# The S5 parameters of a hybrid encoder layer: scratch memory of their own, and a place at the head of the program

## The chip, the cores and the metric

The kernel runs on one core of a Trainium2 chip. The time is that of one execution on the device, in microseconds (us). The engines are TensorE (PE, with its weight loads PEld), VectorE (DVE), ScalarE (ACT), GpSimd (POOL) and SyncE (SP), which issues most transfers. Before the change the median of 3 runs is 1712.62 us (1712.08 to 1717.11).

## What is computed

One layer of a hybrid trunk, for 1024 tokens of a prompt and 32 of a decoded sample, with a width of 1024, all in float32:

```python
h = rmsnorm(x, prm['ln_mix_g'])
z = h @ prm['w_in'] + prm['b_in']                  # mLSTM q k v o i f | attention q k v | S5 u
y_a = head_rmsnorm(jax.nn.sigmoid(o_a) * mlstm(q_a, k_a, v_a, i_a, f_a, c0, n0, m0), prm['gn_a_g'], 4)
y_b = head_rmsnorm(stick_breaking(q_b, k_b, v_b), prm['gn_b_g'], 6)
y_s, s_re, s_im = s5(u_c, prm, s0_re, s0_im)
g = jax.nn.gelu(y_s)
y_c = rmsnorm(g * jax.nn.sigmoid(g @ prm['w_glu'] + prm['b_glu']), prm['gn_c_g'])
x = x + concat(y_a, y_b, y_c) @ prm['w_out']
x = x + cross_attn(rmsnorm(x, prm['ln_x_g']), mem_k, mem_v, prm['w_xq'], prm['w_xo'])
x = x + conv_ffn(rmsnorm(x, prm['ln_ffn_g']), prm, conv_prev)
```

S5 is a diagonal state space model of 16 groups with 64 complex states each and 16 channels. Before it can run, its parameters have to be prepared: from `ssm_a_re`, `ssm_a_im` and `ssm_log_dt` come the step, the magnitude, the sine and cosine of each state's rotation, the first 8 powers of the transition and the rotation squared ten times over; `ssm_b` is scaled with these and `ssm_c` is transposed.

## The kernel before, in words

**Stages.** The nine x tiles (eight of 128 tokens, one of 32) are normed, transposed by PE and split into a high and a low part; each dense product is three matmuls with the halves of both operands. The input projection runs over blocks of 128 output columns and three chunks of tokens. Its first three blocks (u, u, and the gates) run chunk by chunk, so that PE can begin on chunk 0 with three x tiles; the others run block by block, in the order attention 0 and 1, mLSTM 0 and 1, attention 2, mLSTM 2. Then come the keys and values of the memory, `w_out`, the cross attention and the FFN (from about 960 us on).

**The order of the work.** The main stream is those dense products. Beside it run side streams, written as generators: the norms of the x tiles, the parameter columns (`vec_late`, line 638), S5 with its GLU (`s5`, line 1331, `glu`, line 1619), the norm of the memory (`lend`, line 1687), the attention (`stick`) and the mLSTM (`mlstm`, line 1099). A planner (lines 62 to 259) keeps a clock for each engine and a cost for each instruction; after each step of the main stream, `advance` asks every side stream in turn, and one whose inputs are ready by the planner's clock emits its next step. A transfer costs 0.5 us of one shared issue resource and 0.65 us and its bytes at 360 GB/s. All instructions go through one helper, so the profile gives nearly all of them line 173. Behind the planner a scheduler of the compiler places instructions once more, by a simulation of its own: one that was written later but has its operands can go ahead.

**Gates.** S5's groups need u in DRAM; the mLSTM preface needs the gates and `s5_done` (line 1100), its chunks need all twelve mLSTM blocks (line 1202); `w_out` needs attention, S5 and the first mLSTM chunks (line 2065).

**Memory.** `m_s5` (line 533) is a stretch of 8896 columns. x tiles 4 to 8 lie in it from column 3000 on (line 582). `s5` waits until all nine x tiles are normed (line 1332), frees the stretch and takes it again: 2560 columns for the small parameters (`sc`), the rest for the large tiles (`sw`). The raw parameters `pr` and `h0` and the scratch `tq`, `tq2`, `tb` lie in the tile `ot`, and the raw `ssm_c` in `W1`; those are columns in which x tiles lay. `s5`, `vec_late` and the others are added after the eighth step of the first dense blocks (line 1710). `vec_late` loads 11 rows of gains, biases and convolution weights, yields once, and transposes them to the columns `vecC` and `vecB`.

**In the trace**, S5's tiles, x tiles 4 to 8 and the mLSTM's are all `zy`, x tiles 0 to 3 and the attention's `zf`, the split tokens `zb` (high) and `za` (low), and the PSUM tiles `mm`, `tp` and `gp`.

Of the kernel before, what the change touches and what calls it, by code (L numbers as in the profile page):

```python
# [7 lines left out]
F32 = mybir.dt.float32  # L8
# [7 lines left out]
P = 128  # L16
D = 1024
# [10 lines left out]
SG, SC, SP_ = 16, 16, 64  # L28
# [5 lines left out]
NB = TA // 8  # L34
NP_ = T // 8
S5_W = 8896
OUT_AT = [0, 416, 800, TA]
SAMPLE_AT = 2
DEPTH = 4
# [7 lines left out]
SLACK = [-0.25, 1, -0.5]  # L47
# [6 lines left out]
def tile_fn(tc, *args):  # L54
# [7 lines left out]
    clk = {"pe": 0.0, "act": 0.0, "dve": 0.0, "pool": 0.0, "sp": 0.0}  # L62
# [25 lines left out]
    def width(x):  # L88
        n = 1
        for d in x.shape[1:]:  # L90
            n *= d
        return n
# [39 lines left out]
    class Timed:  # L132
        def __init__(self, eng, key):
            self.eng, self.key = eng, key
# [43 lines left out]
    g = Timed(nc.gpsimd, "pool")  # L178
    pe = Timed(nc.tensor, "pe")
# [49 lines left out]
    def add(x, at=None, slack=0.0):  # L229
        sd = x if isinstance(x, Window) else Side(x, chain[0], slack)  # L230
        sides.insert(len(sides) if at is None else at, sd)
        return sd

    def advance():
        for sd in list(sides):
            sd.run()
            if sd.done:
                sides.remove(sd)
# [7 lines left out]
    def until(cond):  # L246
        while not cond():
            t = clk["pe"]
            advance()
            if clk["pe"] == t and not cond():  # L250
                clk["pe"] += 0.25
                assert clk["pe"] < 1e4, "nothing moves"
# [8 lines left out]
    with ExitStack() as top:  # L261
# [34 lines left out]
        class Mem:  # L296
# [39 lines left out]
            def tile(self, shape, dt=F32):  # L336
                x = self.view(shape, dt, self.at)
                self.at += (width(x) + 7) // 8 * 8
                return x
# [26 lines left out]
        def const(shape, dt=F32, name="c"):  # L366
            return cpool.tile(shape, dt, name=name)
# [155 lines left out]
        for gi, grp in enumerate(GROUPS):  # L523
            for n in DOWN if gi == 0 else range(KD):
# [7 lines left out]
        sp = Bag({"ss": (4, 8), "stg": (3, IN_W), "sthl": (2, 2 * IN_W, "R"), "nat": (1, 9 * P)})  # L532
        m_s5 = Mem(S5_W)
        xb = Bag({"g": (1, D), "xt": (4, D), "ur": (2, 8 * NB), "vr": (2, P), "graw": (1, KD * 64),
                  "ghl": (1, KD * P, "R"), "mhl": (2, KD * P, "R")})


        ident = const([P, P], name="ident")
# [40 lines left out]

        xn = [0]  # L580
        gmix = xb.tile([P, D], "g")
        xts = [xb.tile([P, D], "xt") if i < 4 else m_s5.view([P, D], F32, 3000 + (i - 4) * D) for i in range(9)]

        def x_load(i, eng):
            n = P if i < 8 else TS
# [2 lines left out]
        def x_tile(i):  # L588
            yield from norm_T(None, P if i < 8 else TS, gmix, h_hi, h_lo, i * P, xts[i])
            xn[0] = i + 1  # L590
# [14 lines left out]
        ra, rb = xb.tile([P, P], "vr"), xb.tile([88, P], "vr")  # L605
# [32 lines left out]
        def vec_late():  # L638
            at = 0
            for key, ap in (("b_glu", a["b_glu"][0]), ("gn_a", a["gn_a_g"][0]), ("gn_b", a["gn_b_g"][0]),  # L640
                            ("gn_c", a["gn_c_g"][0]), ("ln_x", a["ln_x_g"][0]), ("ln_ffn", a["ln_ffn_g"][0]),
                            ("ln_f", a["ln_f_g"])):
                VA[key] = at
                at = rows(ra, at, ap)
            at = 0
            for j in range(3):
                at = rows(rb, at, a["ffn_conv_w"][0, j])
            rows(rb, at, a["ffn_conv_b"][0])
            yield
            pa, pb = gp(), gp()  # L650
            pe.transpose(pa[:, :34], ra[:34], ident[:34, :34])
            pe.transpose(pb[:, :88], rb, ident[:88, :88])
            v.tensor_copy(vecC, pa[:, :34])
            v.tensor_copy(vecB, pb[:, :88])
            late.append(1)
            yield
# [664 lines left out]
        def cmul(o_r, o_i, ar, ai, br, bi, t0, t1, g_=None):  # L1321
# [6 lines left out]
            v.tensor_tensor(out=o_r, in0=o_r, in1=t0, op=ALU.subtract)  # L1328
            g_.tensor_tensor(out=o_i, in0=o_i, in1=t1, op=ALU.add)

        def s5():
            while xn[0] < 9:
                yield
            G = 4
            tt, ts2 = v.tensor_tensor, v.tensor_scalar
            m_s5.free()
            m_sc, m_sw = Mem(2560), Mem(S5_W - 2560)
            sc, sw = m_sc.tile, m_sw.tile
            tc_, tsn = sw([P, G, NB]), sw([P, G, NB])
            uK, xp, GC, GS = (sw([P, G, NB]) for _ in range(4))  # L1340
            VT, ot, VTt, VJt, W1, TT = (sw([P, G, P]) for _ in range(6))
            Ks = sw([P, G, SC])
            otv = ot.rearrange("p g n -> p (g n)")

            pr = otv[:48, 0:2 * SP_].rearrange("r (j p) -> r j p", j=2)
            for i, nm in enumerate(("ssm_a_re", "ssm_a_im", "ssm_log_dt")):
                for j in range(2):
                    s.dma_start(pr[16 * i:16 * i + 16, j, :], a[nm][0])
            h0 = otv[:32, 2 * SP_:4 * SP_].rearrange("r (j p) -> r j p", j=2)
            s.dma_start(h0[0:16, 0], a["state_ssm_re"][0, 0])  # L1350
            s.dma_start(h0[0:16, 1], a["state_ssm_im"][0, 0])
            s.dma_start(h0[16:32, 0], a["state_ssm_im"][0, 0])
# [3 lines left out]
            sy.dma_start(nA[64:P], a["ssm_b_im"][0].rearrange("g p c -> p g c"))  # L1356
            sy.dma_start(nB[0:64], a["ssm_b_im"][0].rearrange("g p c -> p g c"))
            sy.dma_start(nB[64:P], a["ssm_b_re"][0].rearrange("g p c -> p g c"))
            cn = W1.rearrange("p g n -> p (g n)").rearrange("p (h j i q) -> p h j i q", h=2, j=2, i=2)
            for hf in range(2):  # L1360
                rr = slice(8 * hf, 8 * hf + 8)
                for j, (x, y_) in enumerate((("ssm_c_re", "ssm_c_im"), ("ssm_c_im", "ssm_c_re"))):
# [58 lines left out]
            yield  # L1421

            Lr, Li = sc([P, 16, 9]), sc([P, 16, 9])
            tq = otv[:, 256:320].rearrange("p (g m) -> p g m", g=16)
            tq2 = otv[:, 320:384].rearrange("p (g m) -> p g m", g=16)
            g.memset(Lr[:, :, 0:1], 1.0)
            g.memset(Li[:, :, 0:1], 0.0)
            v.tensor_copy(Lr[:, :, 1], lr)
# [26 lines left out]

            ts2(nB[0:64], nB[0:64], -1.0, None, op0=ALU.mult)
            bA, bB = sc([P, 16, SC]), sc([P, 16, SC])
            tb = otv[:, 0:256].rearrange("p (g c) -> p g c", c=SC)
            bc = [P, 16, SC]
            zrb, zib = zr.unsqueeze(2).to_broadcast(bc), zi.unsqueeze(2).to_broadcast(bc)  # L1460
            tt(out=bA, in0=nA, in1=zrb, op=ALU.mult)
# [26 lines left out]
            fin = sc([P, 2, 2, 16])  # L1488
            X0, X0J = sc([P, 16]), sc([P, 16])
            yield  # L1490
            tE = [otv[:, 256 * i:256 * i + 256].rearrange("p (g n) -> p g n", g=G) for i in range(2)]
            for hf in range(4):
                gs = slice(G * hf, G * hf + G)
# [8 lines left out]
                for i in range(8):  # L1502
                    m = 1 << i
# [75 lines left out]
                for dst, tab in ((GC, tc_), (GS, tsn)):  # L1579
                    v.tensor_tensor(out=dst[:, :, 1:NB], in0=xp[:, :, 0:NB - 1], in1=tab[:, :, 0:NB - 1], op=ALU.mult)  # L1580
                    i = 0 if dst is GC else 1
# [28 lines left out]
            sy.dma_start(p_ssm_im[0, 0], fo[0:16, 64:P])  # L1610
            sy.dma_start(s_ssm_re[0, 0], fo[16:32, 0:64])
            sy.dma_start(s_ssm_im[0, 0], fo[16:32, 64:P])
            m_sc.free()
            m_sw.free()
            yield
            yield from glu()
            s5_done.append(1)
# [1 line left out]
        def glu():  # L1619
            mg = Mem(S5_W)  # L1620
            sg_ = mg.tile
# [56 lines left out]
        chunks = list(range(NCH))  # L1678
        h_free = []
        xw_ = add(Window((x_tile(i) for i in range(9)), 4))  # L1680
        until(lambda: xn[0] >= 1)
        W.prime(1)

# [11 lines left out]

        def later_sides():
            add(vec_late())
            add(s5(), slack=SLACK[0])
            add(lend())
            add(stick())  # L1700
            add(mlstm(), slack=SLACK[1])
# [671 lines left out]

        out_n = [OUT_AT[c + 1] - OUT_AT[c] for c in range(NCH)]
        early, stat_done, out_done = {}, [], []

        def os_(c):
            return slice(OUT_AT[c], OUT_AT[c + 1])

        def out_tiles(c):  # L2380
            end = min(OUT_AT[c + 1], T)
            t = [(t0, min(P, end - t0)) for t0 in range(OUT_AT[c], end, P)]
            return t + [(T, TS)] if c == NCH - 1 else t
# [137 lines left out]
```

## Time and profile before

| | |
|---|---|
| median of 3 runs | 1712.62 us |
| the profiled execution, its own time | 1716.38 us |
| its span in the trace | 1714.6 us |
| PE, PEld busy | 96%, 93% of the span |
| DVE, ACT, POOL busy | 66%, 44%, 27% |
| mean granted clock of PE | 0.987 |
| moved by the DMA engines | 229.91 MB, mean 134 GB/s |

The profile is that of one execution; its rows give the start of an instruction from the span's start, its time, engine, operation, tiles and shapes, and in brackets how long the engine had been idle before it and what ended that. The granted clock is the share of TensorE's full clock that the throttle let through.

### The profile page before, as it was taken

To read this page: it belongs to the slowest core of one execution; us is meant where nothing else is said; L and a number is where in the kernel's file an instruction comes from. 1 tells how busy PE (TensorE), PEld (TensorE's weight loads), DVE (VectorE), ACT (ScalarE), POOL (GpSimd) and SP (SyncE) were. 2 spreads that over 40 slices of the span, in tenths; PEclk is the share of its full clock that TensorE was granted. 3 is DMA by queue.
4 is the path that set the end of the run, shared out by engine and by line. 5 is a ranking of instruction groups with operands and counts; after the bars stand their busy time and mean duration, and the time that the engine had idled before them with its cause. 6 is when DMAs were issued, how large, how long until landed. Compare 5 with 4: busy or idle time off the path is not lost.

```text
span 1714.6 us, 30434 instructions
## 1 busy us (share of the span) xinstructions
PE 1642.7 (96%) x11616; PEld 1598.1 (93%) x11616; DVE 1137.3 (66%) x2209; ACT 753.6 (44%) x1480; POOL 463.2 (27%) x624
## 2 busy tenths in 40 slices
PE   5999999999999799999999989999999999999997
PEld 5989989999888799999999889999999999999997
DVE  6778878845796667766656698777777777333232
ACT  5434434534664555544444454444444445111143
POOL 4234335011214233200102546533333330000022
PEclk9999999999899999999999999999999999999999
DMA  7564544254479965455554555222222217332121
GB/s 216 146 161 115 138 109 105 78 158 133 124 232 257 253 200 162 125 170 178 171 167 124 159 158 169 94 76 89 86 75 75 76 63 240 127 100 75 43 69 65
DMA packets 328392, 229.91 MB, mean 134 GB/s; under 512 B 43564, under 2 KB 309707, under 8 KB 327991
## 3 DMA queue, kind: packets, MB, share of 16 engines
q1 hardware_dynamic: 309991, 214.57, 42.5%
q10 hardware_dynamic: 18256, 13.40, 2.6%
q8 instruction: 92, 1.51, 0.4%
q14 instruction: 53, 0.43, 0.1%
HBM read 170.95 MB, written 56.38 MB: 133 GB/s over the span
## 4 chain that ended last, share of the span: by engine, by line
PE 76%; DMA 9%; DVE 8%; issue 2%; ACT 2%; POOL 1%; SPq 1%; ACTq 0%; DVEq 0%; POOLq 0%
PE mm L173 47%; PE gp L173 19%; PE tp L173 10%; DVE zy L173 3%; DVE zf L173 2%; DVE zr L173 1%; DVE zx L173 1%; DMA d_mv<-zr 1%; DMA zf<-d_act 1%; SPq L173 1%; DVE w_lo L173 1%; DMA w_raw<-in_w_in_dram 1%; ACT zy L173 1%; DMA zy<-d_uu 1%; ACT zf L173 0%
## 5 line engine op out<-in xcount | busy, mean ns | idle before, releaser
L173 PE MATMUL mm<-zb,w_hi 128*128 128x352 f32 (+4 forms) x1234 | 366.5, 330 | 2.5 <-DVE zb L173 1.3
L173 PE MATMUL mm<-zr,w_hi 128*128 128x352 f32 (+2 forms) x1358 | 289.2, 312 | 8.4 <-ACT zf L173 4.1
L173 ACT ACTIVATE w_hi<-w_raw 128x1024 fp32r<-128x1024 f32 (+1 forms) x150 | 149.6, 997 | 284.5 <-PE mm L173 207.2
L173 PE MATMUL mm<-zb,w_lo 128*128 128x384 f32 (+2 forms) x826 | 273.6, 331 | 0.0
L173 POOL TENSOR_TENSOR zf<-zf 128x352 f32<-128x352 f32 (+5 forms) x98 | 118.5, 1210 | 566.5 <-ACT zf L173 484.8
L173 PE MATMUL mm<-zr,w_lo 128*128 128x264 f32 (+2 forms) x1058 | 235.9, 304 | 0.7 <-ACT zf L173 0.7
L173 PEld LDWEIGHTS mm<-zb,w_hi 128*128 128x128 f32 x1234 | 227.6, 190 | 4.3 <-DVE zb L173 1.6
L173 PEld LDWEIGHTS mm<-zr,w_hi 128*128 128x128 f32 x1358 | 216.2, 191 | 10.8 <-ACT zf L173 4.8
L173 DVE TENSOR_TENSOR w_lo<-w_raw,w_hi 128x1024 fp32r<-128x1024 f32 (+1 forms) x127 | 159.8, 1258 | 55.8 <-ACT w_hi L173 55.1
L173 PE MATMUL mm<-za,w_hi 128*128 128x384 f32 (+1 forms) x552 | 184.5, 334 | 0.0
L173 DVE TENSOR_TENSOR zx<-mm,zx 128x352 f32<-128x352 f32 (+3 forms) x120 | 62.7, 523 | 177.7 <-PE mm L173 177.3
L173 PEld LDWEIGHTS mm<-zr,w_lo 128*128 128x128 f32 x1058 | 164.6, 189 | 0.9 <-ACT zf L173 0.9
L173 PEld LDWEIGHTS mm<-zb,w_lo 128*128 128x128 f32 x826 | 157.8, 191 | 0.7
L173 PE MATMUL tp<-ident,zf 128*128 128x128 f32 (+3 forms) x530 | 89.1, 285 | 31.1 <-DVE zf L173 22.2
L173 PE MATMUL mm<-zy,w_hi 128*128 128x352 f32 x456 | 114.1, 326 | 1.6 <-DVE zx L173 1.6
L173 PE MATMUL gp<-zy 128*128 128x132 f32 (+13 forms) x722 | 109.7, 290 | 2.2 <-DVE zg L173 0.9
L173 DVE TENSOR_TENSOR zy<-zy 128x16 f32<-128x16 f32 (+9 forms) x371 | 97.5, 304 | 15.3 <-POOL zy L173 6.7
L173 ACT ACTIVATE zf<-gp 128x512 f32<-128x512 f32 (+6 forms) x180 | 75.6, 476 | 72.2 <-PE gp L173 59.6
L173 PEld LDWEIGHTS mm<-za,w_hi 128*128 128x128 f32 x552 | 106.4, 193 | 0.5
L173 PEld LDWEIGHTS tp<-ident,zf 128*128 128x128 f32 (+3 forms) x530 | 64.3, 146 | 41.7 <-DVE zf L173 20.8
L173 PEld LDWEIGHTS gp<-zy 128*128 128x128 f32 (+6 forms) x722 | 97.1, 186 | 4.9 <-DVE zg L173 1.3
L173 POOL TENSOR_TENSOR zy<-zy 128x16 f32<-128x16 f32 (+8 forms) x123 | 82.3, 680 | 67.7 <-DVE zy L173 56.9
(232 smaller groups left out, 3364.2 us busy)
## 6 DMA issues: line engine op xcount, KB each, us to landing
w_raw<-in_w_ffn_a_dram SPq DMA_DIRECT2D x27, 512.0 KB
w_raw<-in_w_out_dram SPq DMA_DIRECT2D x24, 512.0 KB
w_raw<-in_w_xq_dram SPq DMA_DIRECT2D x24, 512.0 KB
w_raw<-in_w_xo_dram SPq DMA_DIRECT2D x24, 512.0 KB
w_raw<-in_w_in_dram SPq DMA_DIRECT2D x23, 512.0 KB
d_act<-zx SPq DMA_DIRECT2D x22, 528.0 KB
zf<-d_act SPq DMA_DIRECT2D x22, 528.0 KB
w_raw<-in_w_ffn_down_dram SPq DMA_DIRECT2D x16, 512.0 KB
```

The source lines that it names most:

```text
L173: return f(*args, **kw)
```

## The change

Four edits. The prepared parameters get scratch columns in `m_s5` in which no x tile lies: `otp` in columns 2560 to 2944, and the raw `ssm_c` in columns 8120 to 8632, behind x tile 8; the stretch is no longer freed and taken again but cut in two by the small class `Part`. The wait for the nine x tiles moves from the head of `s5` to behind the preparation, ahead of the first group. `s5` is added as a side stream right after the norms of the x tiles, before any dense product. And `vec_late` waits for 30 us of the planner's clock between its loads and its two transposes, which are pinned behind what PE had been given before them.

```diff
+S5_X = 3000
...
             rows(rb, at, a["ffn_conv_b"][0])
-            yield
+            t = clk["pe"]
+            while clk["pe"] < t + 30:
+                yield
             pa, pb = gp(), gp()
-            pe.transpose(pa[:, :34], ra[:34], ident[:34, :34])
-            pe.transpose(pb[:, :88], rb, ident[:88, :88])
+            tc.keep_in_program_order(pe.transpose(pa[:, :34], ra[:34], ident[:34, :34]))
+            tc.keep_in_program_order(pe.transpose(pb[:, :88], rb, ident[:88, :88]))
...
+        class Part:
+            def __init__(self, mem, at, n):
+                self.mem, self.at, self.end = mem, at, at + n
+
+            def tile(self, shape):
+                x = self.mem.view(shape, F32, self.at)
+                self.at += (width(x) + 7) // 8 * 8
+                assert self.at <= self.end
+                return x
+
         def s5():
-            while xn[0] < 9:
-                yield
...
-            m_s5.free()
-            m_sc, m_sw = Mem(2560), Mem(S5_W - 2560)
-            sc, sw = m_sc.tile, m_sw.tile
+            sc, sw = Part(m_s5, 0, 2560).tile, Part(m_s5, 2560, S5_W - 2560).tile
...
-            pr = otv[:48, 0:2 * SP_].rearrange("r (j p) -> r j p", j=2)
+            otp = m_s5.view([P, 384], F32, 2560)
+            cn = m_s5.view([P, 512], F32, S5_X + 5 * D)
+            pr = otp[:48, 0:2 * SP_].rearrange("r (j p) -> r j p", j=2)
...
-            h0 = otv[:32, 2 * SP_:4 * SP_].rearrange("r (j p) -> r j p", j=2)
+            h0 = otp[:32, 2 * SP_:4 * SP_].rearrange("r (j p) -> r j p", j=2)
...
-            cn = W1.rearrange("p g n -> p (g n)").rearrange("p (h j i q) -> p h j i q", h=2, j=2, i=2)
+            cn = cn.rearrange("p (h j i q) -> p h j i q", h=2, j=2, i=2)
...
             X0, X0J = sc([P, 16]), sc([P, 16])
             yield
+            while xn[0] < 9:
+                yield
...
-            m_sc.free()
-            m_sw.free()
+            m_s5.free()
...
         xw_ = add(Window((x_tile(i) for i in range(9)), 4))
+        add(s5(), slack=SLACK[0])
         until(lambda: xn[0] >= 1)
...
             add(vec_late())
-            add(s5(), slack=SLACK[0])
             add(lend())
```

In the same way `tq`, `tq2` and `tb` become views of `otp`.

## Rows read from the trace of the kernel before

**Rows 1.** The page, busy time of each engine.

```profile
PE 1642.7 (96%) x11616; PEld 1598.1 (93%) x11616; DVE 1137.3 (66%) x2209; ACT 753.6 (44%) x1480; POOL 463.2 (27%) x624
```

**Rows 2.** Windows: us, busy PE, PEld, DVE, ACT, POOL (instructions), clock, DMA share, GB/s.

```profile
0.00:25.00 25.00, 9.64 (x40) 7.87 (x41) 13.63 (x21) 15.21 (x26) 17.15 (x42) 1.00 0.81 246
10.00:15.00 5.00, 2.23 (x8) 1.43 (x8) 3.85 (x6) 4.17 (x8) 3.27 (x3) 1.00 1.03 232
15.00:20.00 5.00, 1.30 (x4) 0.73 (x4) 4.31 (x5) 3.11 (x5) 5.00 (x4) 1.00 0.79 278
25.00:50.00 25.00, 22.84 (x147) 21.39 (x146) 15.36 (x27) 11.96 (x24) 3.29 (x5) 1.00 0.48 129
50.00:100.00 50.00, 49.96 (x327) 49.05 (x326) 42.06 (x236) 21.92 (x39) 17.55 (x37) 1.00 0.53 150
```

**Rows 3.** Timeline, parameter transfers on the queues of ACT and SP.

```profile
42.29 0.32 ACTq L173 DMA_DIRECT2D zy<-in_ssm_a_re_dram  x1
50.65 0.44 ACTq L173 DMA_DIRECT2D zy<-in_ssm_c_im_dram  x1
22.16 0.73 SPq L173 DMA_DIRECT2D zy<-in_ssm_b_re_dram  x1
```

**Rows 4.** Windows, instructions that touch tile zy alone, columns as in rows 2.

```profile
50.00:80.00 30.00, 0.50 (x2) 0.27 (x2) 16.12 (x122) 2.36 (x6) 9.31 (x8) 1.00 0.55 158
```

**Rows 5.** Timeline, POOL: a weight split, the first power, the first angle table.

```profile
16.40 2.35 POOL L173 TENSOR_TENSOR w_lo<-w_raw,w_hi 128x1024 fp32r<-128x1024 f32 x1
52.91 2.91 POOL L173 TENSOR_TENSOR zy<-zy 128x16 f32<-128x16 f32 x1 [0.89 <-DVE zy L173]
79.42 0.72 POOL L173 TENSOR_TENSOR zy<-zy 128x4 f32<-128x4 f32 x3 [13.65 <-DVE zy L173]
```

**Rows 6.** Timeline, PE: the transposes of vec_late.

```profile
30.63 0.45 PE L173 MATMUL gp<-ident,zy 34*128 34x34 f32 x2 [2.08 <-DMA zy<-in_ln_ffn_g_dram]
```

**Rows 7.** Readers of vecC, the earliest: ns min/median/max, first and last start us.

```profile
L173 DVE SCALAR_TENSOR_TENSOR zy<-zf,vecC,gp x3: 242/243/248, 164.2 to 455.9; 128x32 f32<-128x32 f32 x3
```

**Rows 8.** Transfers that touch d_u (u in DRAM), columns as in rows 7.

```profile
L173 SPq DMA_DIRECT2D zy<-d_u x16: 303/414/584, 64.5 to 286.5; - x16
L173 SPq DMA_DIRECT2D d_u<-zy x2: 343/405/467, 61.4 to 62.8; - x2
```

**Rows 9.** Timeline, SP: gates for the mLSTM preface, last projection block stored.

```profile
408.41 0.60 SPq L173 DMA_DIRECT2D zy<-d_g  x2
482.29 0.99 SPq L173 DMA_DIRECT2D d_oa<-zf  x2
```

**Rows 10.** Timeline, DVE's preface scans, and PE in and after its two waits.

```profile
419.72 4.70 DVE L173 TENSOR_TENSOR_SCAN zy<-zy 4x1024 f32<-4x1024 f32 x3
428.68 0.51 PE L173 MATMUL tp<-ident,zf 64*128 64x64 f32 x5 [1.57 <-DVE zf L173]
432.64 1.12 PE L173 MATMUL tp<-ident,zf 128*128 128x128 f32 x4 [1.14 <-POOL zf L173]
434.52 0.52 PE L173 MATMUL mm<-za,w_hi 128*128 128x384 f32 x1
434.84 0.52 PE L173 MATMUL mm<-zb,w_lo 128*128 128x384 f32 x1
436.36 0.34 PE L173 MATMUL mm<-za,w_hi 128*128 128x384 f32 x1
436.53 0.33 PE L173 MATMUL mm<-zb,w_lo 128*128 128x384 f32 x1
```

**Rows 11.** Windows around the mLSTM preface, columns as in rows 2.

```profile
380.00:400.00 20.00, 20.00 (x135) 19.07 (x134) 7.66 (x18) 4.34 (x8) 3.63 (x8) 1.00 0.30 83
420.00:440.00 20.00, 17.29 (x104) 16.03 (x103) 18.45 (x23) 6.97 (x14) 6.65 (x4) 0.83 0.53 130
```

**Rows 12.** Window of the attention and S5 groups, columns as in rows 2.

```profile
100.00:300.00 200.00, 191.98 (x1316) 182.16 (x1315) 166.92 (x362) 87.04 (x192) 77.56 (x151) 0.98 0.50 128
```

**Rows 13.** Window at the end of the memory keys and values.

```profile
550.00:600.00 50.00, 37.50 (x293) 35.14 (x293) 29.83 (x62) 25.07 (x76) 14.36 (x15) 0.93 0.94 251
```

More of the change, by code (lines that the diff above doesn't have):

```diff
@@ L581, in tile_fn @@
         gmix = xb.tile([P, D], "g")
-        xts = [xb.tile([P, D], "xt") if i < 4 else m_s5.view([P, D], F32, 3000 + (i - 4) * D) for i in range(9)]
+        xts = [xb.tile([P, D], "xt") if i < 4 else m_s5.view([P, D], F32, S5_X + (i - 4) * D) for i in range(9)]
         def x_load(i, eng):
@@ L1423, in s5 @@
             Lr, Li = sc([P, 16, 9]), sc([P, 16, 9])
-            tq = otv[:, 256:320].rearrange("p (g m) -> p g m", g=16)
-            tq2 = otv[:, 320:384].rearrange("p (g m) -> p g m", g=16)
+            tq = otp[:, 256:320].rearrange("p (g m) -> p g m", g=16)
+            tq2 = otp[:, 320:384].rearrange("p (g m) -> p g m", g=16)
             g.memset(Lr[:, :, 0:1], 1.0)
@@ L1457, in s5 @@
             bA, bB = sc([P, 16, SC]), sc([P, 16, SC])
-            tb = otv[:, 0:256].rearrange("p (g c) -> p g c", c=SC)
+            tb = otp[:, 0:256].rearrange("p (g c) -> p g c", c=SC)
             bc = [P, 16, SC]
```

## The prediction

> **What bounds the kernel now.** I read the page first. TensorE (PE) is busy 96% of the span and DVE 66% [rows 1], so the kernel is PE-bound: a change that adds no matmul and removes none can only win or lose the 72 us in which PE stands idle (1714.6 less 1642.7) and what PE loses while its clock is halved behind a wait. So the question is which of these idle stretches the preparation of S5 causes. The windows come next, to see where the idle time lies and what the other engines do there; then the list of PE's waits; then the timelines of the waits that the edits touch. Of the first 25 us PE works 9.64 and of the next 25 it works 22.84 [rows 2]. The reader is to see that the start is held by transfers and norms (DMA share 1.03 in 10 to 15 us) and that POOL has no room at all from 15 to 20 us (5.00 of 5.00), while from 25 to 50 us DVE has 9.6 us left and POOL 21.7 [rows 2].
>
> **The preparation today.** Its parameters are loaded late. The first small transfer on ACT's queue goes out at 42.29 and the last ends at 51.09 [rows 3], because `ot` and `W1` lie where x tiles 7 and 8 lie. SP's four ssm_b loads already go at 22.16 and after [rows 3]: the compiler's scheduler had moved them. The work runs from 50 to 80 us and beyond: 122 DVE instructions, 16.1 us, in those 30 us alone [rows 4], three powers on POOL of 2.9 us each (the first at 52.91), and the first angle table at 79.42 [rows 5]. But PE is fully busy there (49.96 of 50 us, [rows 2]), so the preparation itself costs PE nothing today. A gain has to come from what follows it, or from the other edit.
>
> **The change, part by part.**
>
> (a) *Later parameter transposes.* PE stands for 2.08 us before the transposes at 30.63, waiting for the load of ln_ffn_g [rows 6]; the matmuls behind them had their operands. The edit puts the pair at least 30 planner-us behind the loads and pins them in PE's order. The two transposes (0.45 us) stay as work. Their first reader comes at 164.2 [rows 7], so nothing waits for them instead. Taken: -2.1 us. Ends: -2.1, and 0 if x tiles 3 to 5 are late anyway and PE waits for them in the same place.
>
> (b) *The preparation moves into the start.* All of it counts: 19 transfers on ACT's queue, of which three are issued at the start today and 16 move; 4 on SP, now right behind the x loads, where they run ahead of the row loads that (a) lets come late; 6 transposes on PE; two sines and one table load on ACT; some 150 small DVE instructions; three powers on POOL. The planner charges each transfer 0.5 us on one shared issue resource. With 18 charged by then (7 x, gain and weight loads, 6 for biases and gate, 5 more x) and 23 of S5, the second step is ready near (18 + 23) x 0.5 + 1.6 = 22 planner-us, and the powers two steps on. That is behind POOL's two weight splits (the second at 16.40, 2.35 us [rows 5]), in the stretch where POOL has 21.7 us and DVE 9.6 us left. The 16.1 us of DVE work exceed that room by 6.5 us, but what doesn't fit runs from 50 us on, as now. PE reaches the second column chunk only after 72 matmuls on the first, some 11 us where 147 instructions take 22.84 [rows 2], so a small delay of x tiles 3 to 8 is hidden. If that cover is gone, the price is between 0 and the three powers standing in POOL's line before an x tile's own power, 8.7 us. A gain is excluded: the x tiles gain no resource. Taken: +1.0 us, near the low end, since the planner places the powers behind the splits.
>
> (c) *S5 ends earlier.* The first of four groups can start when u is in memory; its first loads go out at 64.5, but its tables begin at 79.42 [rows 5, 8]. So the lead is at most 15 us, whatever the preparation saves. It carries to the last group (its first load of u at 286.5 or before [rows 8]), to GLU and to the mLSTM preface, which waits for S5: its load of d_g goes at 408.41 [rows 9]. The mLSTM chunks themselves wait for the last projection, stored at 482.29 [rows 9]; that isn't moved, and it leaves 50 us or more of slack. So the direct way S5 to mLSTM is worth 0. What can be won is where the preface lands. It puts scans of 4 rows x 1056 on DVE, 4.70 us for three [rows 10], and behind them wait two scans of the attention, for which PE waits 1.57 and 1.14 us. After that PE's matmuls follow each other by 0.32 us in place of 0.17 [rows 10]; the granted clock of this window is 0.83 [rows 11], that is, part of it at 1.2 and the rest at 2.4 GHz. I count 15 matmuls at that pace: 15 x 0.15 = 2.3 us. Together 5.0 us. Fifteen us earlier the preface begins near 393, where DVE is busy 7.66 of 20 us and not 18.45 [rows 11]. Taken: -5.0 us. Ends: -5.0, and +2.7 if it meets two scans as it does now and one more wait of the same size is added.
>
> (d) *S5's groups meet the attention at other places.* From 100 to 300 us PE is idle 8.0 us, with DVE at 83% [rows 12]. Each of these waits may go or come when the groups slide by 15 us; no row says which. Taken: 0. Ends: -4 and +4, half of the idle time each way.
>
> Sum: -2.1 + 1.0 - 5.0 + 0 = -6.1 us. The profiled execution took 1716.38 us by its own clock (span 1714.6) and would take 1710.3; the median of the three runs is 3.8 us below it, and the same step from 1712.62 gives **1706.5 us**. A measurement of this kernel tells a difference from no change at about 0.3%, 5.1 us.
>
> The edits without a cost: the scratch views change addresses alone, and the new wait before the groups (all nine x tiles normed) is over before u is stored, at 61.4 [rows 8].
>
> **A rule that speaks against it.** The rows show the 16 DMA engines at a share of 1.03 from 10 to 15 us at 232 GB/s [rows 2], and ACT's transfers now join them. The Trainium skill, "SBUF — State Buffer", section "Can I just issue two DMAs to hit both halves?", says that all DMAs of a kernel land on the same 16 engines and that issuing from several engines doesn't help. No row here shows ACT's parameter loads beside the x loads in number, so whether it holds is open.
>
> **The rivals.**
>
> *R1, only the stall returns.* The preface slides by 15 us and meets other scans at the same price; the lead ends in mLSTM's slack. For it: PE is full from 50 to 100 us and the chunks' gate is the projection. Against it: the empty DVE of 380 to 400 us. Time: 1712.6 - 2.1 + 1.0 = 1711.5. Chance 0.22.
>
> *R2, the engines collide.* Some 0.57 MB of parameters (ssm_b 4 x 64 KB, ssm_c 8 x 32, the rest 56), 0.49 of them new in this place, at 232 GB/s take 2.1 us from the x loads, which hold the start. The start loses what (a) gives: 1706.5 + 2.1 = 1708.6. Chance 0.04. By the page's rule it is this one.
>
> *R3, slower: the powers stand in the way of the norms.* Place: POOL between 10 and 21 us. The scheduler puts instructions by its own simulation, and if parameters land there sooner than x tiles, the powers precede the norms' own powers and the weight splits, and PE's first chunk starts later. Price 8.7 us on the path, and (c) may still fall out as in R1: 1711.5 + 8.7 - 1.0 = 1719.2. It decides when the first power starts before 16 us. Against it: the planner's 22 us. Chance 0.16.
>
> *R4, slower: the cover goes.* If S5 and attention run ahead, less side work is left where PE is already short of it, 550 to 600 us, idle 12.5 us [rows 13]. An estimate, half as much again, is 6.2 us: 1711.5 + 6.2 = 1717.7 or a little more. Chance 0.10.
>
> *R5, it doesn't do what it says.* The scheduler keeps the preparation where it was, and DVE starts it near 50 us: 1712.6 - 2.1 = 1710.5 from the stall alone. Chance 0.03.
>
> **How the numbers follow.** The forecast has the rest, 0.45. Faster by over 0.3% is the forecast, 0.45; within 0.3% are R1, R2 and R5, 0.29; slower are R3 and R4, 0.26. The low end takes (a), (c) and (d) at their best and (b) at 0: 1712.6 - 2.1 - 5.0 - 4.0 = 1701.5; with the half clock that follows two waits of (d), 2 us, 1699.5. The high end reaches R3, 1719.2, and some of R4: 1720. Left out are a little of R3 and R4 with (d) against them, and larger gains. The forecast's own range is 1699.5 to 1707.5.
>
> **What would show it.** Right: no wait for ln_ffn_g in PE's list; the powers between 22 and 45 us; the first angle table near 65; d_g's load 10 to 20 us earlier and no half clock behind the preface. Wrong: a first dense matmul run later than today, where PE works 1.30 us from 15 to 20 and is fed from there on, by more than 2 us (R3, R2); d_g's load unmoved (R5); PE idle more than 12.5 us where the memory keys and values end (R4); the same two waits behind the scans of 4 rows (R1).

## The result: slower, and where the time went

The changed kernel takes **1736.99 us** (median of 4 runs, 1735.07 to 1740.32), the kernel before 1714.74 beside it (4 runs, 1712.08 to 1717.11): a ratio of **1.0132**, 95% interval 1.0107 to 1.0157. I forecast a gain of 6 us, and it loses 22. The profiled execution took 1735.07 us with a span of 1733.3, 18.7 more than the span before.

The page of the changed kernel, busy time of each engine, answers to [rows 1]:

```profile
PE 1656.0 (96%) x11616; PEld 1611.0 (93%) x11616; DVE 1139.6 (66%) x2209; ACT 755.2 (44%) x1480; POOL 448.2 (26%) x624
```

The same 11616 matmul records are 13.3 us longer, and the idle time (span less busy) grew from 71.9 to 77.3 us, by 5.4. So most of the loss isn't waiting: it is the same work, taking longer while the clock is lower. Both are found by place with four windows, of the kernel before first (columns as in [rows 2]):

```profile
0.00:50.00 50.00, 32.48 (x185) 29.26 (x186) 28.99 (x47) 27.17 (x49) 20.43 (x47) 1.00 0.65 187
50.00:400.00 350.00, 341.94 (x2328) 327.52 (x2327) 266.18 (x703) 155.58 (x317) 108.39 (x211) 0.99 0.47 127
400.00:700.00 300.00, 277.97 (x1991) 263.67 (x1990) 212.91 (x351) 169.02 (x390) 78.31 (x85) 0.96 0.69 197
700.00:1700.00 1000.00, 984.59 (x7071) 972.36 (x7070) 626.08 (x1101) 397.26 (x717) 253.00 (x277) 0.99 0.37 116
```

And of the changed kernel:

```profile
0.00:50.00 50.00, 31.11 (x160) 28.65 (x161) 28.56 (x53) 26.73 (x48) 21.82 (x46) 0.93 0.66 190
50.00:400.00 350.00, 343.69 (x2344) 329.56 (x2342) 263.00 (x685) 156.07 (x318) 93.30 (x201) 1.00 0.51 137
400.00:700.00 300.00, 272.70 (x1858) 257.35 (x1859) 201.42 (x335) 161.12 (x376) 75.15 (x94) 0.89 0.65 182
700.00:1700.00 1000.00, 984.07 (x7055) 971.52 (x7054) 637.93 (x1117) 399.08 (x715) 249.75 (x274) 1.00 0.38 117
```

Read the third line of each. I call **loss** of a stretch its idle time plus busy time x (1 - granted clock), the second term being what the same work would have saved at the full clock. From 400 to 700 us that is 22.0 + 278.0 x 0.04 = 33 us before and 27.3 + 272.7 x 0.11 = 57 after. The matmul counts say the same: 1858 records in place of 1991. In the other three stretches, added up in windows of 50 us (the table further down), the two kernels are within 4 us of each other, with both signs. The change was made in the first 80 us; its price is paid 350 us later.

**The start.** The wait for ln_ffn_g [rows 6] is gone, but others have come. The timeline of PE in the changed kernel, its instructions with waits from 13 to 36 us:

```profile
14.66 0.29 PE L174 MATMUL gp<-ident,zy 23*128 23x23 f32 x1 [2.35 <-DMA zy<-in_b_in_dram]
16.79 1.01 PE L174 MATMUL mm<-zb,w_hi 128*128 128x384 f32 x2 [0.79 <-ACT zb L174]
27.79 0.66 PE L174 MATMUL tp<-ident,zy 128*128 128x128 f32 x4 [1.49 <-DVE za L174]
32.97 0.69 PE L174 MATMUL mm<-za,w_hi 128*128 128x384 f32 x1 [4.18 <-DVE za L174]
```

The last is a wait for `za`, the low part of a transposed x tile: what (a) named as its other end, tiles that are late anyway, and longer than the 2.08 us it replaces. It isn't a transfer that makes this tile late. DVE's timeline shows two multiplications of the norms ahead of the step that writes `za`:

```profile
29.84 2.47 DVE L174 SCALAR_TENSOR_TENSOR zy<-zy,zf 128x1024 f32<-128x1024 f32 x2 [0.18 <-POOL zf L174]
32.24 1.87 DVE L174 TENSOR_TENSOR za<-tp,zb 128x512 fp32r<-128x512 f32 x3
```

Behind this wait the clock is down, as the window that answers to the fourth of [rows 2] shows (22.84 busy at 1.00 there):

```profile
25.00:50.00 25.00, 19.34 (x114) 18.25 (x113) 16.23 (x32) 11.99 (x24) 6.00 (x7) 0.86 0.47 118
```

SP's loads of x tiles 4 to 7 go out at 15.49 us, 12.86 before. The timeline shows them first, then on POOL the first power of the preparation and the first angle table:

```profile
15.49 3.26 SPq L174 DMA_DIRECT2D zy<-in_x_prompt_dram  x4
...
46.87 2.91 POOL L174 TENSOR_TENSOR zy<-zy 128x16 f32<-128x16 f32 x1 [7.64 <-DVE zy L174]
...
77.19 0.94 POOL L174 TENSOR_TENSOR zy<-zy 128x4 f32<-128x4 f32 x3 [2.13 <-DVE zy L174]
```

The first power is 6 us earlier than in [rows 5] and the first angle table 2 us. Though the last of its parameter loads is issued before 27 us, the preparation hardly moved.

**S5 and the preface.** Transfers of d_ys (S5's output; SP's queue, count, ns min/median/max, first and last start), the kernel before and the changed kernel:

```profile
L173 SPq DMA_DIRECT2D d_ys<-zy x16: 303/421/1309, 156.2 to 330.5; - x16
L174 SPq DMA_DIRECT2D d_ys<-zy x16: 303/424/761, 132.4 to 352.5; - x16
```

SP's timeline, the preface's load of d_g and the last projection block, which answer to [rows 9]:

```profile
432.21 0.60 SPq L174 DMA_DIRECT2D zy<-d_g  x2
...
499.92 1.24 SPq L174 DMA_DIRECT2D d_oa<-zf  x2
```

S5's first group is 24 us ahead and its last 22 us behind: the lead is not only spent, it has turned round, and the preface comes 24 us later and not 15 earlier. The tables came only 2 us earlier, so it isn't the tables that give S5 a lead of 24 us. The preface lands among longer scans of the attention than before (there 64 x 544 and 128 x 512, at 424.35 and 428.56 us). DVE's timeline there, changed kernel:

```profile
443.75 4.70 DVE L174 TENSOR_TENSOR_SCAN zy<-zy 4x1024 f32<-4x1024 f32 x3
...
449.69 1.47 DVE L174 TENSOR_TENSOR_SCAN zf<-zf 128x640 f32<-128x640 f32 x1
...
456.44 1.74 DVE L174 TENSOR_TENSOR_SCAN zf<-zf 128x768 f32<-128x768 f32 x1
...
463.67 2.00 DVE L174 TENSOR_TENSOR_SCAN zf<-zf 128x896 f32<-128x896 f32 x1
```

PE's waits behind them, and windows around the two:

```profile
453.86 1.97 PE L174 MATMUL tp<-ident,zf 128*128 128x128 f32 x8 [2.38 <-DVE zf L174]
...
466.58 2.13 PE L174 MATMUL tp<-ident,zf 128*128 128x128 f32 x9 [2.60 <-DVE zf L174]
```

```profile
450.00:454.00 4.00, 1.62 (x11) 1.18 (x11) 4.00 (x8) 0.79 (x4) 0.00 (x0) 0.88 0.26 36
454.00:457.00 3.00, 3.00 (x13) 2.61 (x14) 3.00 (x6) 2.63 (x6) 0.49 (x1) 0.50 0.89 197
467.00:471.00 4.00, 2.29 (x10) 1.59 (x8) 3.89 (x4) 3.99 (x8) 0.21 (x4) 0.50 1.01 357
471.00:475.00 4.00, 3.73 (x17) 3.46 (x17) 2.88 (x6) 0.81 (x2) 0.19 (x4) 0.50 1.08 211
```

PE waits, and when its operands are there it works at 1.2 GHz (0.50 of full) though it is fully busy. The stretches of the other rows: 380 to 400 us is as full as before; 420 to 440 is now undisturbed (20.00 busy, clock 1.00, against 17.29 and 0.83 in [rows 11]); 440 to 460 took its place (16.63 at 0.83). From 550 to 600 us [rows 13] PE's idle time fell from 12.5 to 5.3 us while the clock fell from 0.93 to 0.80.

The preface's stretch is about half of it. In windows of 50 us the changed kernel loses 11.7 us more than before from 450 to 500, 5.4 from 500 to 600 and 11.1 from 600 to 700, and gains 3.6 from 400 to 450. The last stretch, before and changed:

```profile
600.00:700.00 100.00, 96.91 (x620) 95.17 (x621) 69.67 (x107) 50.90 (x98) 30.68 (x23) 0.98 0.59 174
600.00:700.00 100.00, 90.69 (x588) 88.54 (x587) 66.64 (x100) 53.62 (x117) 29.62 (x25) 0.93 0.68 196
```

That is where the time goes. Is it the change that does it?

### The profile page after: what moved, and what is told of

Same layout as the page of the kernel before. It is cut to its first block, busy times and chain, and to the rows that moved or that the text cites. A ratio compares the mean times of both kernels' runs of the same rounds, so it can differ in the third digit from the quotient of the medians.

```text
span 1733.3 us, 30451 instructions
## 1 busy us (share of the span) xinstructions
PE 1656.0 (96%) x11616; PEld 1611.0 (93%) x11616; DVE 1139.6 (66%) x2209; ACT 755.2 (44%) x1480; POOL 448.2 (26%) x624
## 4 chain that ended last, share of the span: by engine, by line
PE 75%; DVE 10%; DMA 8%; issue 3%; ACT 2%; POOL 1%; SPq 1%; DVEq 0%; POOLq 0%; ACTq 0%
PE mm L174 46%; PE gp L174 19%; PE tp L174 10%; DVE zy L174 4%; DVE zf L174 2%; DVE zr L174 1%; DVE zx L174 1%; DVE w_lo L174 1%; DMA zy<-d_uu 1%; DMA zf<-d_act 1%; ACT zf L174 1%; DMA d_ya<-zy 1%; ACT zy L174 1%; SPq L174 1%; DMA zr<-d_k 1%
## 5 line engine op out<-in xcount | busy, mean ns | idle before, releaser
L174 POOL TENSOR_TENSOR zf<-zf 128x352 f32<-128x352 f32 (+5 forms) x98 | 114.5, 1170 | 552.5 <-ACT zf L174 488.6
L174 PE MATMUL gp<-zy 128*128 128x132 f32 (+13 forms) x722 | 113.9, 299 | 0.7 <-ACT zf L174 0.7
L174 PE MATMUL tp<-ident,zf 128*128 128x128 f32 (+1 forms) x530 | 90.2, 293 | 19.8 <-DVE zf L174 15.1
L174 DVE TENSOR_TENSOR zy<-zy 128x16 f32<-128x16 f32 (+8 forms) x371 | 99.1, 307 | 13.6 <-POOL zy L174 6.9
L174 PEld LDWEIGHTS gp<-zy 128*128 128x128 f32 (+6 forms) x722 | 101.1, 194 | 3.0 <-ACT zf L174 0.9
L174 POOL TENSOR_TENSOR zy<-zy 128x16 f32<-128x16 f32 (+8 forms) x123 | 76.7, 632 | 77.5 <-DVE zy L174 58.5
L174 PEld LDWEIGHTS tp<-ident,zf 128*128 128x128 f32 (+1 forms) x530 | 67.5, 150 | 27.8 <-DVE zf L174 16.3
```

The costliest lines, as they stand in the source:

```text
L174: return f(*args, **kw)
```

## The experiments

The order of the work isn't written down in this kernel. A planner deals it out by its own clock, and a step that is ready at another time can shift everything behind it. Two theories stood first. **Order**: the loss comes from the order that the planner deals anew behind the change. **Start**: it comes from the preparation running beside the x tiles. What tells them apart is a kernel with the edits and the old order, and one with a new order and none of the edits. Since the planner is part of the program, its times can be written out for each variant without the chip; the expectations quote them.

**One edit at a time.** First the parameter columns alone in the kernel before (the transposes at least 30 planner-us after their loads, and pinned):

```
-            yield
+            t = clk["pe"]
+            while clk["pe"] < t + 30:
+                yield
```

> The kernel before with the edit to vec_late alone; the planner deals out all other work as before (planned times equal within 0.03 us). Order theory (the loss comes from the order that the planner deals anew, S5's last group and the mLSTM preface ending later): 1712 to 1715, my step (a) being worth up to -2.1 us. Start theory (the loss comes from the preparation running beside the x tiles): the same. Pinning theory (the two transposes pinned in TensorE's order hold up what stands behind them): 1720 or more.

Measured: 1719.58 us, ratio 1.0027 (1.0011 to 1.0043). No gain, and no theory had it: above the 1712 to 1715 of two of them, and just under the 1720 of the third. PE's timeline of this run shows what stands in place of the wait of 2.08 us:

```profile
30.37 0.45 PE L173 MATMUL mm<-za,w_hi 128*128 128x384 f32 x1 [0.94 <-DVE za L173]
...
36.66 0.41 PE L173 MATMUL mm<-zb,zr 128*128 128x384 f32 x1 [0.87 <-ACT zy L173]
```

The first is a wait for an x tile, which is late there itself; the second is one for ScalarE. Next the changed kernel without this edit (the reverse diff):

> The changed kernel without its edit to vec_late; planned times equal to the changed kernel's within 0.1 us. Order theory and start theory: 1737 within 3 us, a wait for ln_ffn_g of up to 2.1 us back near 30 us. Pinning theory: 1720 or less.

Measured: 1741.57 us, 1.0156 (1.0132 to 1.0180). So the loss stays without this edit, and the pinning theory falls. The time is 1.6 us above what the two others allowed. The wait for the rows is back, and longer than the 2.1 us expected (PE's timeline of this run):

```profile
34.41 0.29 PE L174 MATMUL gp<-ident,zy 34*128 34x34 f32 x1 [4.54 <-DMA zy<-in_ffn_conv_w_dram]
36.23 0.38 PE L174 MATMUL gp<-ident,zy 88*128 88x88 f32 x1 [1.53 <-DMA zy<-in_ffn_conv_b_dram]
```

SP's four ssm_b loads go out from 24.24 us on in this run, ahead of the row loads (29.84 to 34.62); in the kernel before the rows' loads run from 16.71 to 26.57. So inside the change edit (a) does take something away: without it the first 50 us lose 6.9 us more than before, with it 3.5. In the medians that is 4.6 us, and the intervals overlap.

**The edits with the old order.** The memory is apart, S5 is added in its old place and waits for the nine x tiles, and the planner is shown the old columns, so that every step gets its old time to the hundredth:

```
+        for n_, a_, b_, d_ in shift:
+            if nm == n_ and a_ <= lo and hi < b_:
+                lo, hi = lo + d_, hi + d_
```

> Memory apart as in the change, so the compiler's scheduler and the chip may start the preparation early, but the planner is told of the old columns and so deals out every step at exactly the times of the kernel before; vec_late as before. Order theory: 1713 to 1719, the start costing at most the 2 to 4 us by which the first chunks' evictions came later in the changed kernel; the preface's load of d_g within 5 us of 408.4. Start theory: 1728 or more, with the parameters' transfers before 22 us.

Measured: 1717.82 us, 1.0008 (0.9988 to 1.0027): no difference. All 19 of ACT's small transfers go out between 0.74 and 22.4 us, as in the changed kernel, and d_g is loaded at 409.2. But the compiler's scheduler put the first power later, not earlier, so this run tests the transfers and the memory, not the early work (POOL's timeline of this run):

```profile
56.69 2.91 POOL L178 TENSOR_TENSOR zy<-zy 128x16 f32<-128x16 f32 x1 [15.66 <-DVE zy L178]
```

With the columns edit added to it:

> The run e5_plan_kept with the later, pinned parameter transposes added: all the memory and column edits of the change, with every other step planned where it was before (within 0.05 us). If the edits add up: 1714.9 + 1.3 (memory, e5_plan_kept) + 4.1 (columns, e1_columns_late) = 1720, within 3 us. If the columns' cost in e1_columns_late was an accident of that program: 1713 to 1718. Start theory, if the missing part of it was the columns: 1730 or more.

Measured: 1717.39 us, 1.0008 (0.9999 to 1.0018). The time lies in both of the first two ranges; the ratio is that of e5_plan_kept, so the 4 us of e1_columns_late don't show again, though intervals of this width can't exclude most of them.

The early work was still open. In the next two kernels the preparation's instructions are emitted early without being charged, and the planner charges them later, where the kernel before had them, without emitting them:

```
+                if mode[0] == "emit":
+                    return f(*args, **kw)
...
-                return f(*args, **kw)
+                return None if mode[0] == "plan" else f(*args, **kw)
```

> The whole change (memory apart, later columns, the preparation's instructions emitted at the planner's times of the changed kernel), while the planner charges the preparation where the kernel before had it, so that every other step is planned as before (within 0.04 us). Any-new-order theory: 1715 to 1721, the start costing up to 4 us. Start theory: 1730 or more.

> Memory apart, columns as before, and the preparation's steps emitted one after the other from the planner's 30.6 us on, 1.2 us apart (its last before 50), all other steps planned as before. The first power should come before 46 us. Any-new-order theory: 1715 to 1722, with what the start loses (PE idle and half clock up to 50 us, 17.5 us before) up by 0 to 6 us. Start theory: 1730 or more, as the preparation now collides with the x tiles more than in the changed kernel.

Measured: e14_whole_order_kept 1718.34 us, **1.0019** (1.0003 to 1.0035); e15_prep_at_once, which leaves out edit (a), 1723.96, 1.0046 (1.0032 to 1.0059), 2 us above the order theory's range and 6 below the start theory's. The first power in POOL's timeline of e14_whole_order_kept, and two of its windows:

```profile
51.90 2.91 POOL L170 TENSOR_TENSOR zy<-zy 128x16 f32<-128x16 f32 x1 [12.36 <-DVE zy L170]
```

```profile
0.00:50.00 50.00, 30.65 (x157) 28.11 (x158) 29.26 (x46) 27.05 (x48) 17.16 (x45) 0.93 0.67 190
...
400.00:700.00 300.00, 276.99 (x2007) 263.35 (x2006) 210.16 (x351) 169.38 (x389) 79.32 (x89) 0.97 0.70 199
```

The timeline of e15_prep_at_once, PE's longest wait behind its first transpose and the first power, and its windows:

```profile
33.80 0.29 PE L184 MATMUL gp<-ident,zy 34*128 34x34 f32 x1 [4.94 <-DMA zy<-in_ln_f_g_dram]
...
42.84 3.96 POOL L170 TENSOR_TENSOR zy<-zy 128x16 f32<-128x16 f32 x1 [1.47 <-DVE zy L170]
```

```profile
0.00:50.00 50.00, 28.33 (x143) 25.63 (x144) 28.56 (x62) 25.78 (x46) 25.73 (x47) 0.90 0.67 190
...
400.00:700.00 300.00, 276.88 (x1980) 263.71 (x1980) 206.68 (x345) 167.77 (x386) 80.52 (x89) 0.95 0.69 198
```

The whole change with the old order costs 0.2% and not 1.3%, and from 400 to 700 us it loses 23.0 + 277.0 x 0.03 = 31 us, no more than before.

In e15_prep_at_once the preparation really is early (10 us ahead of before, 4 ahead of the changed kernel): the first 50 us lose 21.7 + 28.3 x 0.10 = 24.5 against 17.5 before, 7.0 more where 6 was the most expected, near the 8.7 us that the medians show. But its long wait is for a row load, the one that edit (a) avoids, and e4_columns_as_before, also without (a), loses 6.9 there with its first power at 50.71. With (a) in, the first 50 us lose 2.2 us more than before where the preparation stays late (e11_plan_kept_columns) and 3.5 to 5.8 where it is given out early: 3.5 in the changed kernel, 4.0 in e14_whole_order_kept, 5.0 in e10_early_old_columns (below), whose first power is the earliest of all at 40.89. So, by one execution of each, the early transfers cost some 2 us, early work 1 to 4 more, and neither gains anything. In the changed kernel the first power lies between those of e14 and e15.

**New orders, none or little of the change.** Three variants of the kernel before. The preface held back; the planner's first margin, by which a next step of S5 and its GLU counts as ready, moved by 0.05 us one way and the other (`SLACK = [-0.2, 1, -0.5]`, `[-0.3, 1, -0.5]`):

```
-            while "gate" not in avail or not s5_done:
+            while "gate" not in avail or not s5_done or clk["pe"] < 400:
```

> The kernel before with the mLSTM preface held until the planner's clock reads 400 us (about 20 us later than before); all that is planned ahead of it is unchanged, and the planned end of the first layer's part is 1592.7 us against 1592.8. Preface theory (the changed kernel loses because the preface meets the longer attention scans): 1725 to 1737, the loss at 440 to 500 us. Any-new-order theory (every order dealt anew loses, because the planner charges no half clock after a wait and this kernel's margins were picked on one order): 1720 to 1745, the loss spread over 440 to 700 us. Planned-end theory (the time follows the planner's own end): 1715 within 3 us.

> The kernel before with one number changed, the first margin of the planner from -0.25 to -0.2 us: nothing of the change is in it, the start is the same, and the order behind it is dealt anew (S5's last step planned at 387.8 us, as in the changed kernel; planned end 1599.5 against 1592.8). Any-new-order theory: 1725 to 1745. Planned-end theory: 1722 within 3 us. Start theory: 1715 within 5 us.

> The kernel before with the planner's first margin at -0.3 in place of -0.25 us: nothing of the change in it, the order unchanged up to about 300 us and dealt anew behind it (S5's last step planned at 385.4, planned end 1597.1). Any-new-order theory: 1722 to 1745, all of the loss behind 300 us. Planned-end theory: 1719 within 3 us. If the loss needs a new order at the start of the attention: 1715 within 3 us.

Measured: e7_preface_later 1728.02 us, 1.0071 (1.0050 to 1.0092); e8_slack 1732.22, 1.0092 (1.0058 to 1.0125); e12_slack3 1732.11, 1.0098 (1.0079 to 1.0116). All three lose where the changed kernel does. On the chip e7_preface_later moved the preface's scans by 4.6 us alone (424.30, 419.72 before), and 8.4 of its 9.4 us lie between 600 and 700. The window of e12_slack3:

```profile
400.00:700.00 300.00, 267.38 (x1901) 255.02 (x1900) 200.83 (x328) 164.14 (x380) 71.38 (x83) 0.94 0.69 192
```

That is 32.6 + 267.4 x 0.06 = 49 us, 16 over the kernel before, without a single edit of the change.

**New orders of the changed kernel.** S5's first group held to 104 or 95 planner-us (`while xn[0] < 9 or clk["pe"] < 104:`); the planner shown the old columns, while the preparation is emitted in the changed kernel's place (the planner's second step of it at 37.9 us, 46.9 in the changed kernel); the preface held to 425; the first margin at -0.1.

> The changed kernel with one more condition: S5's first group isn't emitted before the planner's clock reads 104 us, about where the kernel before emits it. The preparation and the whole start are those of the changed kernel; what follows is dealt anew (S5 planned to end at 366.7 us, 388.0 in the changed kernel). Order theory: some other time, 1712 to 1730, and the start (first chunk's evictions) as slow as in the changed kernel. Start theory: 1737 within 4 us.

> The changed kernel with S5's first group held until the planner's clock reads 95 us; preparation and start as in the changed kernel, S5's last step planned at 376.3 us (388.0 in the changed kernel, 380.2 before), planned end 1591.1. Any-new-order theory: 1725 to 1750. Planned-end theory: 1713 plus the 2 to 4 us of the start. Start theory: 1737 within 4 us. Preface theory: 1720 or less, as the preface lies ahead of that of the kernel before.

> The changed kernel, but the planner is told of the parameters' old columns, so that it plans the preparation as if it waited for x tiles 7 and 8; the program's memory and the place of the emission are those of the changed kernel. The order behind is dealt anew: S5's last step planned at 359.9 us, planned end 1588.9, the earliest of all. Any-new-order theory: 1720 to 1750. Planned-end theory: 1711 plus the 2 to 4 us of the start. Preface theory: 1718 or less.

> The changed kernel with the mLSTM preface held until the planner's clock reads 425 us (388 in the changed kernel); start and S5 are those of the changed kernel. Preface theory: TensorE's loss between 440 and 500 us (idle and half clock) falls from some 18 us to under 10, and the time to 1722 to 1732. Any-new-order theory: another loss elsewhere in its place, 1725 to 1750.

> The changed kernel with the planner's first margin at -0.1 in place of -0.25 us; start as in the changed kernel, order behind dealt anew (S5's last step planned at 385.2, planned end 1589.4). Any-new-order theory: anywhere from 1715 to 1750, most likely 1725 to 1745. Planned-end theory: 1712 plus the start's 2 to 4 us.

Measured: e6_groups_held 1746.92 us, 1.0181 (1.0155 to 1.0207), above what either theory had said (I had bounded a new order by the loss already seen); e9_hold95 1748.36, 1.0182 (1.0148 to 1.0216); e10_early_old_columns 1738.97, 1.0141 (1.0097 to 1.0184); e13_preface_after_attention 1746.95, 1.0189 (1.0173 to 1.0204); e16_other_margin 1738.03, 1.0133 (1.0109 to 1.0156). None of them is faster than the changed kernel beyond the intervals, and none comes near the kernel before.

All together, loss of each run by the windows of its profile (idle + busy x (1 - clock), summed over windows of 50 us, so a little finer than the single lines above), as difference to the kernel before in us; "rest" is 700 to 1700; the planned end is the planner's own clock at the end of the program. Each row is one execution, and behind the first 50 us the five of the old order differ from it by up to 4.5 us, so less than that is not read:

| run | order | planned end | ratio | 0-50 | 50-400 | 400-700 | rest |
|---|---|---|---|---|---|---|---|
| e1_columns_late | old | 1592.7 | 1.0027 | -0.4 | -1.5 | +4.5 | -1.0 |
| e5_plan_kept | old | 1592.8 | 1.0008 | +2.6 | -3.1 | +0.5 | +1.2 |
| e11_plan_kept_columns | old | 1592.7 | 1.0008 | +2.2 | -2.7 | -4.2 | +2.8 |
| e14_whole_order_kept | old | 1592.7 | 1.0019 | +4.0 | +0.4 | -2.8 | -1.3 |
| e15_prep_at_once | old | 1592.8 | 1.0046 | +7.0 | -2.6 | +2.7 | -2.2 |
| changed kernel | new | 1593.8 | 1.0132 | +3.5 | -3.2 | +24.6 | -4.0 |
| e4_columns_as_before | as changed | 1593.8 | 1.0156 | +6.9 | -3.4 | +23.5 | +0.1 |
| e7_preface_later | new | 1592.7 | 1.0071 | -0.6 | +2.1 | +9.4 | +0.7 |
| e8_slack | new | 1599.5 | 1.0092 | -0.2 | -5.3 | +19.7 | +0.1 |
| e12_slack3 | new | 1597.1 | 1.0098 | +1.0 | +3.1 | +14.8 | +0.2 |
| e6_groups_held | new | 1595.3 | 1.0181 | +5.8 | +8.4 | +21.4 | -1.5 |
| e9_hold95 | new | 1591.1 | 1.0182 | +4.3 | +0.7 | +20.9 | -1.4 |
| e10_early_old_columns | new | 1588.9 | 1.0141 | +5.0 | +3.3 | +21.4 | -0.4 |
| e13_preface_after_attention | new | 1602.3 | 1.0189 | +5.8 | -1.5 | +25.5 | -1.0 |
| e16_other_margin | new | 1589.4 | 1.0133 | +5.3 | +0.6 | +19.8 | -1.8 |

What follows:

- **The start theory falls** as the main cause. With the old order, the edits cost 0.1 to 0.5%, and where the preparation's transfers are early, what they cost lies in the first 50 us.
- **The order theory holds.** Nine new orders lose 9 to 26 us between 400 and 700 us; the five kernels with the old one lose at most 4.5 there. Three of the nine hold none of the edits. What all nine share is the stretch from 600 to 700 us, 4.7 to 19.4 us of the loss (at most 2.3 with the old order); 450 to 500, where the changed kernel's preface lies, holds 10 to 12 us in the changed kernel, e4_columns_as_before, e8_slack and e13_preface_after_attention, and at most 2.9 in the others. All nine move S5 or the preface; no run deals only the attention or the mLSTM chunks anew.
- **The preface alone isn't it.** Held back in the changed kernel (on the chip its scans came only 5.6 us later, at 449.30) it didn't remove the waits: 450 to 500 us kept 9.8 us idle at a clock of 0.83 (8.6 at 0.77 in the changed kernel), and the time rose. In e10_early_old_columns and e6_groups_held the preface's load lies ahead of the one before (392.0 and 405.5 us), and they are slower than the changed kernel or equal to it.
- **The planned end says nothing**: the two earliest planned ends (1588.9, 1589.4) are at 1.4% and 1.3%, the two latest of the kernel before with one margin moved (1597.1, 1599.5) at 1.0 and 0.9%. The plan charges no half clock, and its ends lie within 14 us of each other.

No run beats the kernel before. Of the ten orders measured, its own is the only one without that loss. No run shows why: that its margins had been picked on this order, as the expectation of e7_preface_later has it, would explain it. Open stays which meetings of steps make an order dear, from 600 to 700 us above all, whether a better one than the old exists for the changed kernel, and why e1_columns_late, whose plan is the old one, reads 0.3% slower.

## Why the prediction was wrong, step by step

**(a), -2.1 us taken, no gain measured alone.** The wait went, as said; but its other end was the true one. Alone it leaves waits of 0.94 and 0.87 us, in the changed kernel 4.18. Inside the change it does avoid something that the prediction didn't count, the longer wait for the rows behind the ssm_b loads (6.07 us in e4_columns_as_before). That the matmuls behind them had their operands, which I had read beside [rows 6], held only behind that wait of 2 us; without it they wait themselves.

**(b), +1.0 us taken, +3.5 measured in the changed kernel.** The end of 8.7 holds. Wrong was the planner's 22 us for the second step. Written out, it is planned at 46.9 (49.0 before). First, a step that is added is taken as ready only at the end of the last load planned so far, 26.8, and its first turn came at 30.6; my sum began at zero. Second, the planner notes memory in cells of 32 columns, and 8120 is no multiple of 32: the eight ssm_c loads of 64 columns share cells there, and each is planned behind the one before it, issued from 28.8 to 44.4, some 2.2 us apart and not 0.5. Eight columns further on, at 8128, the planner has the second step at 33.8. So the preparation was planned late again by the change's own address, and the first power came at 46.87 and not between 22 and 45; where the planner was shown the old columns, which start on a cell, it came at 40.89 (e10_early_old_columns). An earlier preparation would have won nothing by the runs above.

**(c), -5.0 us taken: the step that failed, and (d) with it.** "It carries to the last group" was the assumption, and the trace shows the contrary: a lead of 24 us in the first group, larger than the 15 that I allowed, is a lag of 22 in the last. The preface went 24 us the other way. I treated the work behind the change as a train that slides; the planner deals each step by its own readiness, and no lead has to last.

**(d), 0 taken, ends -4 and +4.** Here belongs the loss: +24.6 us from 400 to 700 us. I had the mechanism (groups meet the attention elsewhere) and bounded it by half of the idle time from 100 to 300 us [rows 12]. Both the place and the price were wrong. That stretch gained 3.4 us of busy PE (195.37 of 200 us), and what follows 400 us lost seven times that. Of the 24.6 us, 5.3 are idle time and 19.3 the lower clock; my prices counted 2.3 us of the clock for a whole stall.

**The rivals.** R1: the same waits did return, at 453.86 and 466.58, but at 2.38 and 2.60 us, with more behind them. R2: SP's loads of x tiles 4 to 7 do go out 2.6 us later, and its 2.1 us are near the +2.6 of e5_plan_kept; but its sign didn't come, as PE works 4.21 us from 15 to 20 us, 1.30 before [rows 2], and the first long dense run starts at 20.01, 22.42 before. The rows don't show full engines either: their share from 10 to 15 us is 0.70, not 1.03. So whether the rule of the Trainium skill ("SBUF — State Buffer", section "Can I just issue two DMAs to hit both halves?") decides here stays open. R3 fell: no power comes before 40 us in any of the runs. R4 had the place of a part of the loss, not its form: idle time there fell. R5 was half true: the work moved by 6 us. The number 1719.2 of R3 and the range's end of 1720 were the nearest; no case of mine allowed 22 us, because none asked what the planner does with a later part of the kernel. In the terms of the sum, (c) and (d) together were to give -5.0 us and gave a loss of some 20.

## What to carry to other kernels

Where a planner or a scheduler deals the order, a small edit is two changes: the edit, and a new order of all that follows. Measure the second by itself before you judge the first: move a margin of the planner by a trifle, and see how far the time moves (here 0.9 and 1.0%); then make the edit with the order held, and see what is left (here 0.2%). And look at what the planner itself sees of the edit: here an address that isn't a multiple of its cell moved a step by 13 of its own us. A bound for "it meets other work elsewhere" has to come from such runs, not from the idle time of one good order.

## What was not expected of the hardware

The lower clock can cost as much as the waits. From 400 to 700 us the changed kernel is idle for 27.3 us and gives away 30.0 by its lower clock, the kernel before 22.0 and 11.1; in the window from 454 to 457 us PE is busy for all of 3.00 us at a granted clock of 0.50, behind a stretch of 4 us in which it had worked 1.62. A list of waits, read alone, shows less than half of the loss in this stretch; the granted clock by windows shows the rest.
